# The last feed-forward's first four feature blocks: computed with tokens in rows from eight 512-column weight units, six of them converted before the sub-layer starts

## The chip, the cores and the metric

The kernel runs on one core of a Trainium2 chip. The metric is the device time of one execution in microseconds (us). The engines named below are TensorE (PE, with its weight loads PEld), VectorE (DVE), ScalarE (ACT), and SyncE (SP), which issues nearly all loads.

## The reference, cut to what matters

A trunk of two layers works on 256 latent tokens and 256 context tokens, 1024 features each, in fp32. Each layer is a half-step SwiGLU feed-forward, a block of parallel token mixers, and another half-step feed-forward:

```
def swiglu(x, w_gate, w_up, w_down):
    return (jax.nn.silu(x @ w_gate) * (x @ w_up)) @ w_down

def modulated_norm(x, mod, k, norm_g):
    return rms_norm(x, norm_g[2 * k]) * (1 + mod[:, :, 3 * k + 1]) + mod[:, :, 3 * k]

def gated_residual(x, y, mod, k, norm_g, weight):
    return x + weight * mod[:, :, 3 * k + 2] * rms_norm(y, norm_g[2 * k + 1])

def half_ffn(x, mod, k, norm_g, w):
    h = modulated_norm(x, mod, k, norm_g)
    return gated_residual(x, swiglu(h, *w), mod, k, norm_g, FFN_RESIDUAL)
```

The feed-forward has 2816 hidden features. Only the latent stream is returned, so the last mixer's second half and the last feed-forward run on the 256 latent tokens alone.

## The kernel before, in words

**Arithmetic.** Every fp32 operand of a large product is split into a high and a low part. ACT rounds it to the high part (line 162 for weights, 188 for activations), DVE subtracts that from the original (lines 163 and 189). `mm3` then makes three matmuls of each product, high by high, high by low and low by high (lines 193 to 195).

**Weights** come in units of 512 KB, [128 partitions, 1024 floats]. `run_tasks` walks a list of tasks, each with the units it needs. It loads up to three units ahead into four `raw` buffers (SP, line 152) and converts two ahead into five `hi` and five `lo` buffers. Larger activations live in 13 "slots" of 2064 floats per partition.

**Order.** Each engine takes its instructions in the order of its queue. That order is fixed when the program is built: a scheduler places instructions by the order in which they are written, and what stands under `urgent()` is put earlier, past other work that is ready. SP's loads are one such queue: a load that waits for its buffer holds up the loads behind it.

**The stretch of the change** is the end of the second layer's mixer and the start of the last feed-forward. The 256 tokens are two blocks of 128, tb0 and tb1.

- The mixer's merge makes u (`uhi`, `ulo`) from eight feature blocks. Then the residual X is loaded back from memory into a slot (`unspill`, line 883).
- `closing` makes the out-projection: tb0's first 512 columns (4 units, 24 matmuls of 512 columns), the second 512 columns of tb0 and then of tb1 (4 units held for both), and tb1's first 512 columns (4 units again). That is 96 matmuls.
- After each block's second half comes its chain: the square sums (ACT line 561), the product with the gate (DVE 563), 1/sqrt in small DVE steps (570, 210 to 219), the residual (DVE 574), the next norm's square sum (ACT 446), 1/sqrt again, and the normalised rows xn (DVE 451).
- `prenorm` turns xn to feature rows by 16 transposes on PE (line 468), four to a PSUM tile, each tile with two features of both blocks. It scales and shifts them 256 columns at a time (DVE 476, ACT 478) and splits them. With one stream `turn()`, which calls `prenorm`, stands behind tb1's chain, since each tile needs both blocks.
- The feed-forward then runs one weight unit per task: `gu(f, w)` holds 128 features of the gate (w = 0) or up (w = 1) weights as PE's stationary operand and streams the 256 tokens, 24 matmuls of 256 columns. silu is on ACT (603), the product on DVE (606). Eight such units make the first four of 22 feature blocks.

## Time and profile before

| what | value |
|---|---|
| median of three runs | 2246.11 us (2245.7 to 2246.91) |
| the profiled execution | 2245.83 us |
| its span in the trace | 2244.0 us |
| mean granted TensorE clock | 0.992 |
| PE busy | 97% of the span |
| DVE, ACT busy | 69%, 44% of the span |

The span is the part of the execution that the trace covers. [...] The "busy" shares are means over very different stages, so the stretch of the change has to be read by itself.

### The profile page before, as it was taken

To read this page: it belongs to the slowest core of one execution; us is meant where nothing else is said; L and a number is where in the kernel's file an instruction comes from. 1 tells how busy PE (TensorE), PEld (TensorE's weight loads), DVE (VectorE), ACT (ScalarE), POOL (GpSimd) and SP (SyncE) were. 2 spreads that over 40 slices of the span, in tenths; PEclk is the share of its full clock that TensorE was granted. 3 is DMA by queue.
4 is the path that set the end of the run, shared out by engine and by line. 5 is a ranking of instruction groups with operands and counts; after the bars stand their busy time and mean duration, and the time that the engine had idled before them with its cause. 6 is when DMAs were issued, how large, how long until landed. Compare 5 with 4: busy or idle time off the path is not lost.

```text
span 2244.0 us, 30646 instructions
## 1 busy us (share of the span) xinstructions
PE 2186.8 (97%) x11666; PEld 1833.2 (82%) x11666; DVE 1546.0 (69%) x2760; ACT 997.9 (44%) x1594; POOL 135.4 (6%) x100
## 2 busy tenths in 40 slices
PE   7999999999999999999999999999999999998998
PEld 4877777787888888888878788777778888997997
DVE  4987775778576775664444378878858887876556
ACT  3322223545577833542222253222236468855444
POOL 0000000013152000000000000000000152000000
PEclk9999999999999999999999999999999999998999
DMA  7765564321213334434434236555744214565664
GB/s 285 226 197 182 165 200 146 123 94 68 92 51 113 122 120 143 142 112 133 139 104 134 101 118 197 189 187 181 222 138 152 85 67 126 183 217 173 193 190 155
DMA packets 127555, 334.52 MB, mean 149 GB/s; under 512 B 12840, under 2 KB 26216, under 8 KB 126640
## 3 DMA queue, kind: packets, MB, share of 16 engines
q1 hardware_dynamic: 112240, 315.60, 43.4%
q10 hardware_dynamic: 15168, 16.97, 2.4%
q8 instruction: 91, 1.49, 0.3%
q14 instruction: 56, 0.46, 0.1%
HBM read 322.48 MB, written 10.04 MB: 148 GB/s over the span
## 4 chain that ended last, share of the span: by engine, by line
PE 89%; DVE 6%; ACT 2%; issue 1%; DMA 1%; ACTq 0%; DVEq 0%
PE ps L193 27%; PE ps L194 27%; PE ps L195 27%; PE ps L1259 1%; PE ps L1058 1%; PE ps L1228 1%; PE ps L366 1%; DVE lo L163 1%; PE ps L1073 1%; PE ps L468 1%; PE ps L1075 1%; PE ps L1016 1%; DVE sm L1020 1%; DMA slot<-in_w_ada_dram 1%; PE ps L1019 1%
## 5 line engine op out<-in xcount | busy, mean ns | idle before, releaser
L162 ACT ACTIVATE hi<-raw 128x1024 fp32r<-128x1024 f32 (+1 forms) x444 | 457.4, 1032 | 770.7 <-PE ps L194 255.9
L193 PE MATMUL ps<-slot,hi 128*128 128x512 f32 (+1 forms) x2232 | 778.4, 351 | 6.0 <-ACT slot L188 4.9
L194 PE MATMUL ps<-slot,hi 128*128 128x512 f32 (+1 forms) x2232 | 775.6, 348 | 0.7 <-DVE slot L189 0.5
L195 PE MATMUL ps<-slot,lo 128*128 128x512 f32 (+1 forms) x2232 | 773.6, 347 | 0.0
L163 DVE TENSOR_TENSOR lo<-raw,hi 128x1024 fp32r<-128x1024 f32 (+1 forms) x444 | 526.7, 1190 | 232.3 <-ACT hi L162 230.6
L193 PEld LDWEIGHTS ps<-slot,hi 128*128 128x128 f32 x2232 | 420.5, 189 | 75.9 <-ACT slot L188 6.2
L195 PEld LDWEIGHTS ps<-slot,lo 128*128 128x128 f32 x2232 | 421.5, 189 | 57.4
L194 PEld LDWEIGHTS ps<-slot,hi 128*128 128x128 f32 x2232 | 421.5, 189 | 56.3 <-DVE slot L189 2.0
L193 PE MATMUL ps<-hi,slot 128*128 128x512 f32 (+2 forms) x1048 | 400.3, 382 | 1.9 <-ACT slot L188 1.1
L195 PE MATMUL ps<-hi,slot 128*128 128x512 f32 (+2 forms) x1048 | 398.8, 381 | 0.0
L194 PE MATMUL ps<-lo,slot 128*128 128x512 f32 (+2 forms) x1048 | 398.8, 381 | 0.0
L358 DVE SCALAR_TENSOR_TENSOR t<-raw,sc,t 128x1024 f32<-128x1024 f32 x224 | 280.3, 1281 | 129.9 <-DMA raw<-in_w_ada_dram 129.7
L1046 POOL TENSOR_SCALAR t<-t,sm 128x512 f32<-128x512 f32 (+1 forms) x96 | 135.2, 1420 | 1748.1 <-DVE sm L1043 1693.2
L193 PEld LDWEIGHTS ps<-hi,slot 128*128 128x128 f32 x1048 | 197.1, 188 | 46.2 <-issue 6.6
L195 PEld LDWEIGHTS ps<-hi,slot 128*128 128x128 f32 x1048 | 196.7, 188 | 39.8
L194 PEld LDWEIGHTS ps<-lo,slot 128*128 128x128 f32 x1048 | 197.0, 188 | 38.9 <-issue 0.2
L188 ACT ACTIVATE slot<-t 128x512 fp32r<-128x512 f32 (+1 forms) x138 | 80.5, 594 | 172.3 <-DVE t L606 153.5
L606 DVE TENSOR_TENSOR t<-ps,t 128x512 f32<-128x512 f32 (+1 forms) x88 | 54.7, 622 | 86.5 <-PE ps L195 85.2
L189 DVE TENSOR_TENSOR slot<-t,slot 128x512 fp32r<-128x512 f32 (+1 forms) x138 | 87.6, 643 | 5.1 <-ACT slot L188 4.6
L1020 DVE TENSOR_REDUCE sm<-ps 128x1 f32<-128x512 f32 (+1 forms) x96 | 54.1, 593 | 29.6 <-PE ps L1019 29.0
L603 ACT ACTIVATE t<-ps 128x512 f32<-128x512 f32 (+1 forms) x88 | 46.4, 527 | 24.2 <-DVE t L426 16.5
L189 DVE TENSOR_TENSOR t<-ps,t 128x512 fp32r<-128x512 f32 x80 | 54.2, 684 | 1.9 <-ACT t L188 1.7
(195 smaller groups left out, 1667.7 us busy)
## 6 DMA issues: line engine op xcount, KB each, us to landing
raw<-in_w_gu_dram SPq DMA_DIRECT2D x176, 512.0 KB
raw<-in_w_ada_dram SPq DMA_DIRECT2D x128, 512.0 KB
raw<-in_w_down_dram SPq DMA_DIRECT2D x92, 512.0 KB
raw<-in_w_fm_dram SPq DMA_DIRECT2D x64, 512.0 KB
raw<-in_w_br_dram SPq DMA_DIRECT2D x24, 512.0 KB
raw<-in_w_out_dram SPq DMA_DIRECT2D x24, 512.0 KB
slot<-in_w_ada_dram SPq DMA_DIRECT2D x16, 512.0 KB
raw<-in_w_down_dram SPq DMA_DIRECT2D x20, 256.0 KB
```

Source lines behind the costliest of these rows:

```text
L162: self.nc.scalar.activation(out=hi, in_=raw, func=AF.Copy)
L163: self.nc.vector.tensor_tensor(out=lo, in0=raw, in1=hi.bitcast(F32), op=ALU.subtract)
L188: self.nc.scalar.activation(out=hi, in_=src, func=AF.Copy)
L189: self.nc.vector.tensor_tensor(out=lo, in0=src, in1=hi.bitcast(F32), op=ALU.subtract)
L193: mm(out, lh, rh, start=start, stop=False, **kw)
L194: mm(out, lh, rl, start=False, stop=False, **kw)
L195: mm(out, ll, rh, start=False, stop=stop, **kw)
L358: v.scalar_tensor_tensor(out=acc, in0=units[0], scalar=c, in1=acc, op0=ALU.mult, op1=ALU.add)
L603: nc.scalar.activation(out=hs["sg"][:, :W], in_=ps[:, :W], func=AF.Silu)
L606: nc.vector.tensor_tensor(out=hid[:, :W], in0=ps[:, :W], in1=hid[:, :W], op=ALU.mult)
L1020: v.tensor_reduce(out=mx[:, e:e + 1], in_=ps[:, :nkey], axis=AX.X, op=ALU.max)
L1046: nc.gpsimd.tensor_scalar(out=t[:, :nkey], in0=t[:, :nkey], scalar1=r[:, e:e + 1], scalar2=None, op0=ALU.mult)
```

## The change

- The feed-forward's first eight `gu` units are replaced by eight `gt` units from a new weight array, the first 512 gate and then up columns, in pieces of two 128-feature input blocks by 512 columns.
- `rows_first` takes the tokens of one block as stationary operand and streams the weights: 48 matmuls of 512 columns for tb0, then `pre(1)`, which is tb1's norm, then 48 for tb1. A block's product is [128 tokens, 512 features]. silu and the product act on it whole, four transposes turn it to feature rows, and it is split straight from PSUM.
- `prenorm_block` makes the norm of one token block: two PSUM tiles of four transposes each, each scaled in four pieces of 128 x 128 (two on DVE, two on ACT), then split. It is urgent. `turn()` is called ahead of the last two out-projection tasks of tb1.
- The first six `gt` units are loaded and converted ahead into slots, three among the last merge tasks and three among tb0's first out-projection tasks. The last two come through the ordinary `hi` and `lo` buffers.
- `pair` lays a high and a low part of 256-token width into one slot. u, the last feed-forward's input and its hidden features take half the slots, and the six units take the slots set free.

```
+    def pair(self, W):
+        if 8 * W > SLOT:
+            return self.slot([P, 4, W], F32R), self.slot([P, 4, W], F32R)
+        t = self.slot([P, 2, 4, W], F32R)
+        return t[:, 0], t[:, 1]
...
+    def prenorm_block(self, l, k, tb, st):
...
+        with self.urgent():
+            for c4 in range(2):
+                pt = self.psum()
+                h = self.t512()
+                for i in range(4):
+                    nc.tensor.transpose(pt[:, i * P:(i + 1) * P], xn[:, (4 * c4 + i) * P:(4 * c4 + i + 1) * P], self.ident)
+                for i in range(4):
+                    o, p = h[:, i * P:(i + 1) * P], pt[:, i * P:(i + 1) * P]
...
+                    if i % 2:
+                        nc.scalar.activation(out=o, in_=p, func=AF.Identity, scale=sc, bias=sh)
+                    else:
+                        nc.vector.tensor_scalar(out=o, in0=p, scalar1=sc, scalar2=sh, op0=ALU.mult, op1=ALU.add)
+                sl = slice(tb * P, (tb + 1) * P)
+                self.split(st["hi"][c4][:, :, sl], st["lo"][c4][:, :, sl], h.rearrange("p (c t) -> p c t", c=4))
...
-                if i == nu - TURN and tbs is gb and len(streams) > 1:
+                if i == nu - TURN and tbs is gb:
                     turn()
...
+            def rows_first(units, hs=hs):
+                units = list(rest) + list(units)
+                for tb in range(2):
+                    if tb:
+                        pre(tb)
+                    pss = [self.psum() for _ in range(2)]
+                    sl = slice(tb * P, (tb + 1) * P)
+                    for n, u in enumerate(units):
+                        w, g = divmod(n, 4)
+                        for x in range(2):
+                            kk = 2 * g + x
+                            self.mm3(pss[w], st["hi"][kk // 4][:, kk % 4, sl], st["lo"][kk // 4][:, kk % 4, sl],
+                                     u[0][:, x, :], u[1][:, x, :], kk == 0, kk == NK - 1)
...
+                    g = self.t512()
+                    nc.scalar.activation(out=g, in_=pss[0], func=AF.Silu)
+                    nc.vector.tensor_tensor(out=g, in0=pss[1], in1=g, op=ALU.mult)
+                    pt = self.psum()
+                    for f in range(4):
+                        nc.tensor.transpose(pt[:, f * P:(f + 1) * P], g[:, f * P:(f + 1) * P], self.ident)
+                    self.split(hs["hi"][0][:, :, sl], hs["lo"][0][:, :, sl], pt.rearrange("p (f t) -> p f t", f=4))
...
-        out += mrg[2]
+        early = [[t] for t in ahead]
+        out += weave(mrg[2], sum(early[:3], []))
...
+        end = self.closing(st, qs, False, keys, mm, done, turn)
+        return out + weave(end[:4], sum(early[3:], [])) + end[4:]
```

Where the order moves, first on SP around the load of X (`slot` from `spill`). Before, it stands behind the fourth out-projection unit:

```order
L152 DMA raw_17386<-in_w_fm_dram 128x1024
L152 DMA raw_17388<-in_w_out_dram 128x2x512
L152 DMA raw_17440<-in_w_out_dram 128x2x512
L152 DMA raw_17494<-in_w_out_dram 128x2x512
L152 DMA raw_17496<-in_w_out_dram 128x2x512
L883 DMA slot_17594<-spill_84 128x2048
L152 DMA raw_17546<-in_w_out_dram 128x2x512
```

After the change:

```order
L163 DMA raw_17492<-in_w_out_dram 128x2x512
L163 DMA raw_17501<-in_w_out_dram 128x2x512
L163 DMA raw_17503<-in_w_gt_dram 128x1024
L163 DMA raw_17553<-in_w_out_dram 128x2x512
L163 DMA raw_17603<-in_w_gt_dram 128x1024
L163 DMA raw_17612<-in_w_out_dram 128x2x512
L945 DMA slot_17607<-spill_84 128x2048
L163 DMA raw_17625<-in_w_gt_dram 128x1024
L163 DMA raw_17636<-in_w_out_dram 128x2x512
```

Three `gt` units now stand among the out-projection's loads, the last of them between X and the fifth out-projection unit. X's slot was fresh before. After the change it is one of those that held the mixer's normalised input, which PE reads until the last of the merge's gate products.

On DVE, at the out-projection of tb0, before (189 is the last split of u, 163 a unit's low part, 563 the two halves of tb0 multiplied with the gate):

```order
L189 TENSOR_TENSOR slot_17391<-slot_16182,slot_17390 128x256
L163 TENSOR_TENSOR lo_17651<-raw_17613,hi_17650 128x1024
L163 TENSOR_TENSOR lo_17655<-raw_17625,hi_17654 128x1024
L563 TENSOR_TENSOR slot_17648<-ps_17602,slot_17592 128x512
L163 TENSOR_TENSOR lo_17659<-raw_17637,hi_17658 128x1024
L563 TENSOR_TENSOR slot_17648<-ps_17674,slot_17592 128x512
```

And after (204, 178 and 599 are the same three lines):

```order
L204 TENSOR_TENSOR slot_17393<-slot_16182,slot_17393 128x256
L178 TENSOR_TENSOR slot_17650<-raw_17625,slot_17650 128x1024
L178 TENSOR_TENSOR lo_17656<-raw_17636,hi_17655 128x1024
L599 TENSOR_TENSOR slot_17670<-ps_17614,slot_17605 128x512
L178 TENSOR_TENSOR lo_17673<-raw_17642,hi_17672 128x1024
L178 TENSOR_TENSOR lo_17679<-raw_17653,hi_17678 128x1024
L178 TENSOR_TENSOR lo_17683<-raw_17659,hi_17682 128x1024
L178 TENSOR_TENSOR lo_17687<-raw_17676,hi_17686 128x1024
L599 TENSOR_TENSOR slot_17670<-ps_17702,slot_17605 128x512
```

Before, the seventh to ninth out-projection units (of twelve) are converted between the last split of u and the second 563. After, the sixth `gt` unit and the fifth to ninth out-projection units are. Between that second product and tb0's xn (451 before, 466 after) stand eight more conversions in both kernels.

On PE, between tb0's and tb1's matmuls, after the change (208 to 210 are the three matmuls of `mm3`, 701 turns tb0's hidden features, 512 turns tb1's norm):

```order
L208 MATMUL ps_17910<-hi_17891,slot_17815 128x512
L209 MATMUL ps_17910<-lo_17892,slot_17815 128x512
L210 MATMUL ps_17910<-hi_17891,slot_17815 128x512
L701 MATMUL ps_17964<-ident,t_3122_17961 128x128
L512 MATMUL ps_17971<-ident,t_3108_17889 128x128 x4
L512 MATMUL ps_17983<-ident,t_3108_17889 128x128 x4
L701 MATMUL ps_17964<-ident,t_3122_17961 128x128 x3
L208 MATMUL ps_17995<-slot_17271,slot_17814 128x512
```

Before, there is no such place: all transposes of the norm (468) stand ahead of the first feed-forward matmul, and 192 matmuls follow without one between. Now the first of the transposes of tb0's hidden features stands ahead of those of tb1's norm, and all twelve ahead of tb1's first matmul.

On DVE at the end of the new part, after the change (698 is the product of silu and up for tb1, 519 a scale step, 204 a split):

```order
L519 TENSOR_SCALAR t_3127_17984<-ps_17983,Amod_8896,modT_8895 128x128
L204 TENSOR_TENSOR slot_17814<-t_3125_17972,slot_17814 128x4x128
L204 TENSOR_TENSOR slot_17815<-t_3127_17984,slot_17815 128x4x128
L178 TENSOR_TENSOR lo_18089<-raw_17905,hi_18088 128x1024
L698 TENSOR_TENSOR t_3130_18045<-ps_17996,t_3130_18045 128x512
L178 TENSOR_TENSOR lo_18123<-raw_17907,hi_18122 128x1024
L204 TENSOR_TENSOR slot_17959<-ps_18048,slot_17959 128x4x128
```

The conversion of the second `gu` unit that follows (`lo_18089`) stands ahead of tb1's product. On PE, tb1's four transposes (701) stand behind that product and ahead of the next units' matmuls.

## Rows read from the trace of the kernel before

**Rows 1.** The page, busy time of each engine (share of the span).

```profile
PE 2186.8 (97%) x11666; PEld 1833.2 (82%) x11666; DVE 1546.0 (69%) x2760; ACT 997.9 (44%) x1594; POOL 135.4 (6%) x100
```

**Rows 2.** The page, the chain of work that ended last, by engine.

```profile
PE 89%; DVE 6%; ACT 2%; issue 1%; DMA 1%; ACTq 0%; DVEq 0%
```

**Rows 3.** Waits of PE from 1850 us: us in total, times, longest.

```profile
PE ps L468 <- DVE t L451: 11.2, 2, 6.3
```

**Rows 4.** PE's timeline: start, us, instructions, [idle before <- releaser].

```profile
2013.98 0.39 PE L193 MATMUL ps<-hi,slot 128*128 128x512 f32 x1
...
2035.97 0.39 PE L195 MATMUL ps<-hi,slot 128*128 128x512 f32 x1
2042.65 1.11 PE L468 MATMUL ps<-ident,t 128*128 128x128 f32 x4 [6.29 <-DVE t L451]
2048.63 2.82 PE L468 MATMUL ps<-ident,t 128*128 128x128 f32 x12 [4.87 <-DVE t L451]
2051.43 1.44 PE L193 MATMUL ps<-slot,hi 128*128 128x256 f32 x5
2052.66 0.37 PE L194 MATMUL ps<-slot,hi 128*128 128x256 f32 x1
```

**Rows 5.** DVE's timeline, the chains of tb0 and tb1.

```profile
2026.01 0.69 DVE L563 TENSOR_TENSOR slot<-ps,slot 128x512 f32<-128x512 f32 x1 [2.67 <-ACT t L561]
...
2037.41 0.68 DVE L563 TENSOR_TENSOR slot<-ps,slot 128x512 f32<-128x512 f32 x1
...
2041.84 0.75 DVE L451 TENSOR_SCALAR t<-slot,sm 128x1024 f32<-128x1024 f32 x1
...
2047.82 0.75 DVE L451 TENSOR_SCALAR t<-slot,sm 128x1024 f32<-128x1024 f32 x1
```

**Rows 6.** Instruction groups from 1900 to 2060: busy us, mean ns, idle before.

```profile
L163 DVE TENSOR_TENSOR lo<-raw,hi 128x1024 fp32r<-128x1024 f32 x48 | 58.3, 1222 | 12.8 <-ACT hi L162 12.6
L162 ACT ACTIVATE hi<-raw 128x1024 fp32r<-128x1024 f32 x48 | 50.7, 1058 | 27.9 <-PE ps L194 9.2 <-issue 5.7 <-DMA raw<-in_w_om_dram 2.7
...
L1241 ACT ACTIVATE t<-slot,ZN 128x128 f32<-128x128 f32 x38 | 13.0, 388 | 0.0
...
L189 DVE TENSOR_TENSOR slot<-t,slot 128x512 fp32r<-128x512 f32 x6 | 4.1, 689 | 0.7 <-ACT slot L188 0.6
...
L188 ACT ACTIVATE slot<-t 128x512 fp32r<-128x512 f32 x6 | 3.7, 629 | 2.3 <-DVE t L990 2.3
...
L1270 DVE TENSOR_SCALAR slot<-ps,sm 128x128 f32<-128x128 f32 x8 | 2.8, 344 | 0.0
```

**Rows 7.** SP's timeline: issues of X's load and of out-projection units.

```profile
2003.20 0.46 SPq L883 DMA_DIRECT2D slot<-spill  x1
2007.81 13.42 SPq L152 DMA_DIRECT2D raw<-in_w_out_dram  x8
```

**Rows 8.** Windows: us, busy us by engine, PEclk, DMA share, GB/s.

```profile
2003.00:2011.00 8.00, 8.00 (x70) 8.00 (x69) 5.86 (x10) 4.52 (x7) 0.00 (x0) 1.00 0.90 326
2011.00:2020.00 9.00, 9.00 (x54) 7.87 (x52) 7.04 (x11) 6.57 (x9) 0.00 (x0) 1.00 0.71 237
```

**Rows 9.** Windows with the granted clock (PEclk), the closing and an earlier stage.

```profile
2039.00:2040.00 1.00, 0.00 (x0) 0.00 (x0) 1.00 (x1) 0.87 (x1) 0.00 (x0) 0.60 0.77 274
2040.00:2052.00 12.00, 4.49 (x18) 3.71 (x19) 9.12 (x28) 3.15 (x7) 0.00 (x0) 0.50 0.36 122
2052.00:2053.00 1.00, 1.00 (x8) 1.00 (x7) 0.72 (x3) 1.00 (x3) 0.00 (x0) 0.57 0.00 0
...
528.00:530.00 2.00, 2.00 (x7) 1.55 (x7) 1.10 (x2) 1.11 (x2) 2.00 (x2) 0.50 0.80 287
...
1799.00:1801.00 2.00, 2.00 (x16) 1.78 (x15) 1.92 (x7) 1.17 (x4) 0.72 (x1) 1.00 0.00 0
```

**Rows 10.** PE's timeline, two gaps of nearly equal length.

```profile
526.49 0.39 PE L1073 MATMUL ps<-t,slot 128*128 128x256 f32 x1 [2.18 <-ACT t L1034]
...
1798.31 0.39 PE L1073 MATMUL ps<-t,slot 128*128 128x256 f32 x1 [2.19 <-DVE t L189]
```

More of the change, by code (lines that the diff above doesn't have):

```diff
@@ L46 @@
 N_HI = 5
+N_EARLY = 6
 LA_DMA = 3
@@ L159, in cvt_unit @@
         n = int(np.prod(shape))
-        hi = self.wp.tile([P, n], F32R, tag="hi", name=self.nm("hi"))
-        lo = self.wp.tile([P, n], F32R, tag="lo", name=self.nm("lo"))
+        if key[0] == "gt" and key[4]:
+            both = self.slot([P, 2, n], F32R)
+            hi, lo = both[:, 0, :], both[:, 1, :]
+        else:
+            hi = self.wp.tile([P, n], F32R, tag="hi", name=self.nm("hi"))
+            lo = self.wp.tile([P, n], F32R, tag="lo", name=self.nm("lo"))
         self.nc.scalar.activation(out=hi, in_=raw, func=AF.Copy)
@@ L177, in run_tasks @@
                     nd += 1
-                ready[ncv] = self.cvt_unit(raws.pop(ncv))
+                ready[ncv] = self.cvt_unit(raws.pop(ncv), keys[ncv])
                 ncv += 1
@@ L483, in prenorm @@
             self.split(dh, dl, hv)
+    def prenorm_block(self, l, k, tb, st):
+        nc = self.nc
+        M = self.L[l]
+        if "hi" not in st:
+            st["hi"], st["lo"] = zip(*[self.pair(2 * P) for _ in range(2)])
+        xn = st["xn"][tb]
+        with self.urgent():
[6 more added lines that the diff above has]
+                    o, p = h[:, i * P:(i + 1) * P], pt[:, i * P:(i + 1) * P]
+                    sc, sh = M["A"][:, k, 4 * c4 + i, 0:1], M["modT"][:, 6 * k + c4, i, 0:1]
+                    if i % 2:
+                        nc.scalar.activation(out=o, in_=p, func=AF.Identity, scale=sc, bias=sh)
+                    else:
+                        nc.vector.tensor_scalar(out=o, in0=p, scalar1=sc, scalar2=sh, op0=ALU.mult, op1=ALU.add)
+                sl = slice(tb * P, (tb + 1) * P)
+                self.split(st["hi"][c4][:, :, sl], st["lo"][c4][:, :, sl], h.rearrange("p (c t) -> p c t", c=4))
     def y_half(self, st, tb, n):
@@ L534, in fn @@
                     post(tbs, 0, tbs is gb)
-                    if tbs is gb and len(streams) == 1:
-                        turn()
             return ([keys[0][i]], fn)
@@ L591, in open_hidden @@
                 if "hi" not in hs:
-                    hs["hi"] = [self.slot([P, 4, W], F32R) for _ in range(2)]
-                    hs["lo"] = [self.slot([P, 4, W], F32R) for _ in range(2)]
+                    hs["hi"], hs["lo"] = zip(*[self.pair(W) for _ in range(2)])
             def mms(ps, u, a, b, kks=range(NK), start=True, **kw):
@@ L643, in early_half @@
                 return fn
+            def rows_first(units, hs=hs):
[11 more added lines that the diff above has]
+                                     u[0][:, x, :], u[1][:, x, :], kk == 0, kk == NK - 1)
+                    if not tb:
+                        open_hidden(hs)
+                    g = self.t512()
[5 more added lines that the diff above has]
+                    self.split(hs["hi"][0][:, :, sl], hs["lo"][0][:, :, sl], pt.rearrange("p (f t) -> p f t", f=4))
             first = 0
+            if part == 0 and len(streams) == 1:
+                first = 8
+                out.append(([("gt", l, n // 4, n % 4, False) for n in range(N_EARLY, 8)], rows_first))
             if part == 0 and len(streams) > 1:
@@ L828, in k_cols, with mixer_tasks @@
             R["K"].append(K)
-    def mixer_tasks(self, l, need_ctx, ms, pre, done, turn):
+    def mixer_tasks(self, l, need_ctx, ms, pre, done, turn, ahead):
         nc = self.nc
@@ L942, in mm @@
                 self.mm3(ps, lh, ll, u[0][:, x, :], u[1][:, x, :], k == 0, k == NK - 1)
-        return out + self.closing(st, qs, False, keys, mm, done, turn)
+        end = self.closing(st, qs, False, keys, mm, done, turn)
+        return out + weave(end[:4], sum(early[3:], [])) + end[4:]
     def conv_task(self, l, c, ms, R, need_ctx):
@@ L1342, in fn @@
                 if n == 2 and j % 4 == 0:
-                    R.setdefault("uhi", []).append(self.slot([P, 4, W], F32R))
-                    R.setdefault("ulo", []).append(self.slot([P, 4, W], F32R))
+                    for q, t in zip(("uhi", "ulo"), self.pair(W)):
+                        R.setdefault(q, []).append(t)
                 units = list(units)
@@ L1419, in turn @@
         return (lambda: pre(n + 1)(0)) if n < 5 else (lambda: None)
+    early_units = []
+    ahead = [([("gt", 1, n // 4, n % 4, True)], lambda units: early_units.extend(units)) for n in range(N_EARLY)]
     B.consts()
@@ L1432 @@
         if kind == "mix":
-            tasks += B.mixer_tasks(l, l == 0, states[n], pre(n), done(n), turn(n))
+            tasks += B.mixer_tasks(l, l == 0, states[n], pre(n), done(n), turn(n), [] if l == 0 else ahead)
             continue
-        sub = B.ffn_tasks(l, k // 2, k, streams(n), states[n], pre(n), done(n), turn(n), first[1] if n == 0 else None, rest)
+        sub = B.ffn_tasks(l, k // 2, k, streams(n), states[n], pre(n), done(n), turn(n), first[1] if n == 0 else None, rest if n == 0 else early_units)
         head = 4 if n else 4 + 1 + 3 * FIRST + len(first[1])
@@ L1466, in _layout @@
     a["w_gu"] = c(gu.reshape(2, 2, 2, NK, P, NF, P).transpose(0, 1, 5, 2, 4, 3, 6))
+    gt = np.stack([f["ffn_w_gate"][1, 1, :, :512], f["ffn_w_up"][1, 1, :, :512]])
+    a["w_gt"] = c(gt.reshape(2, NK, P, 512).transpose(0, 2, 1, 3))
     a["w_down"] = f["ffn_w_down"]
```

7 lines of the change are left out of this document (6 added, 1 removed).

## The prediction

> **What bounds the kernel now.** The engine shares come first: PE is busy 97% of the span [rows 1], and the chain that ended last runs 89% on PE [rows 2]. So time is gained only where PE waits, or where it does less work. PE's work doesn't shrink: before, the eight units are 192 matmuls of 256 columns, after, 96 of 512. What is left is PE's waiting, so the waits of PE are read next. In the last 394 us PE waits 11.2 us for xn, in two waits [rows 3]. The timeline places them: 6.29 us ahead of the first four transposes and 4.87 us ahead of the other twelve [rows 4].
>
> All times below are counted from T0 = 2013.98, the first out-projection matmul [rows 4]. The 96 matmuls of 512 columns start 0.2315 us apart ((2035.97 - 2013.98) / 95), and 256 columns take half of that, 0.1157. So before, the out-projection ends at T0+22.2, the first feed-forward matmul starts at T0+37.45 (2051.43), and the eight units end at 2052.66 + 187 x 0.1157 = 2074.3, T0+60.3. This last point is the same point in both programs, because the same `gu` units follow. I work out where it lands.
>
> Why PE waits is in DVE's timeline: tb0's second half is multiplied with its gate at 2026.01, and xn of tb0 is done at 2042.59 [rows 5]. Between stand eight conversions of 1.22 us each [rows 6], 9.8 of 16.6 us. The first wait is DVE's queue. The second is tb1's chain: 2037.41 to 2048.57, 11.2 us [rows 5].
>
> **Supply of the out-projection.** X's load was issued at 2003.20, T0-10.8 [rows 7]. Now its slot is free only after the last merge block's gate product has read it. That block is 24 gate matmuls and then 12 more of 256 columns, so the slot comes free between T0-2.8 and T0-1.4. SP's queue stands still until then, and behind X wait the sixth `gt` unit and the fifth out-projection unit. These 2.1 MB take 6.4 us at the 326 GB/s seen when X and units were loaded together [rows 8], and land at T0+3.6 to 5.0. Conversion adds 1.06 on ACT and 1.22 on DVE [rows 6]: T0+5.9 to 7.3. PE wants it at about T0+5.8 (after 24 matmuls). I take a stall of 0.85 us. The bounds are 0 and, at the 237 GB/s of the next window [rows 8] (8.9 us), 4.0.
>
> **tb0's chain.** In the built order five matmuls of tb1 stand among tb0's second half. It ends at T0+11.1+1.15+0.85 = T0+13.1, where it was T0+11.1. From there to xn it took 17.5 us, and I take 17.0, since the same eight conversions still stand between and DVE has less slack. So xn is ready at T0+30.1. The out-projection ends at T0+23.05. **PE's first wait isn't removed: 7.1 us for 6.3.** Packing and early units don't touch it, since the conversions that fill DVE here are those of later units.
>
> **tb0's norm.** The clock has fallen to 0.50 in the first wait before [rows 9], and does so again. Eight transposes at half clock take 1.9 (2.82 / 12 each [rows 4]). Then come the scale steps: two of 0.344 on DVE beside two of 0.388 on ACT per tile (nearest rows, 128 x 128 [rows 6]), which adds about 0.75 behind the last transpose. The split is 0.63 and 0.69 [rows 6]. In sum 3.95 us: matmuls run from T0+34.1. The bounds are 2.8 (what it took before from twelve transposes to the first matmul [rows 4]) and 5.0, since the out-projection's second product of tb1 (0.68 [rows 5]) and its square sum stand in between. Here is the gain: from xn to the first matmul was 8.85 us, with tb1's chain inside, and is 3.95, so **-4.9**.
>
> [...]
>
> **tb0's matmuls.** 48 x 0.2315 = 11.1. Before, PE ran steadily from 2048.63 and the clock was full at about 2052.66, 4.0 us later [rows 4, 9]. I take the same 4.0 us at half clock, which costs 2.0. So tb0 ends at T0+47.2. tb1's chain hides behind it: its gate product now stands behind three scale steps of tb0 (about T0+32.8), plus 11.2 is T0+44. The second wait is gone.
>
> **The gap to tb1.** PE's next instruction is the first transpose of tb0's hidden features. It needs the product of up with silu, a 128 x 512 step from PSUM (0.69 [rows 5]): PE is idle 0.75 us. Behind it in the queue stand tb1's eight norm transposes, though xn has been ready for 3 us, and three more: twelve, 1.35 us. Then PE waits for two scale steps and the split, 0.69 + 0.63 + 0.69, 2.05 us. So the new gap is 4.15 us, with 2.8 idle, and tb1 runs from T0+51.35 to T0+62.45. The bounds are 2.7 (the high part alone, scale steps hidden) and 5.5 (scale and split of both tiles one after the other).
>
> **The clock in that gap.** Two gaps of 2.18 and 2.19 us ended differently: behind one the clock was 0.50, behind the other 1.00 [rows 9, 10]. This gap is longer in sum but broken by transposes. If it drops, 4 us at half clock cost 2.1. I take the drop, because 2.8 of 4.15 us are idle. [...]
>
> **The tail.** Before, the next units' matmuls follow without a gap. Now tb1's four transposes stand ahead of them. They need the product (0.69), which on DVE stands behind a conversion whose `hi` buffer comes free only 6 matmuls (1.4 us) before tb1's end: 1.06 + 1.22 ends 0.9 after it. Then 0.69 and four transposes, 0.46: 2.05 us, so T0+64.5. Bounds 1.2 (no conversion) and 3.0.
>
> **The sum.** tb0's first matmul 3.35 earlier (T0+34.1 for 37.45), which is -4.9 and 1.55 of lateness. Then: more half clock (2.0, before about 0.6 in the matmuls) +1.4, the gap +4.1, the tail +2.05. That is T0+64.5 for 60.3, **+4.2**; with the clock's drop in the gap **+6.3**. Behind this point PE didn't wait before, and the units are the same. In the merge PE is saturated, and the three early conversions there fit beside it (ACT idle, DVE busy 5.86 of 8.0 us [rows 8]); without that cover each costs up to 1.22. The profiled execution took 2245.83 us, which makes 2252.1; the median shown lies 0.28 higher, so 2252.4.
>
> **The rivals.**
>
> - *A, the forecast*: the clock drops in the gap, 2252.4. Chance 0.40.
> - *B, no drop there*: 2250.3. For it, the 2.19 us gap without one. Chance 0.25.
> - *C, supply*: X's load (1 MB) and three `gt` units (1.5 MB) more in the closing slow all units. At 237 GB/s the fifth unit comes 2.5 us later, and with it tb0's whole chain: 2254 to 2257. For it, the DMA share was 0.90 when X was loaded [rows 8]; against, it was 0.71 in the next 9 us. Chance 0.12.
> - *D, the small losses stay near their lower bounds*: no stall (-0.85), first matmul after 2.8 (-1.15), gap 2.7 (-1.4), tail 1.2 (-0.8), no drop: 2246.1 to 2247, no change. Each has a row for it, but all have to hold. Chance 0.13.
> - *E, the other side*: the eight conversions no longer hold up tb0's xn. Without them the chain is 17.5 - 9.8 = 7.7 us, xn is ready at T0+20.8, before the out-projection ends, so the first wait goes, and the clock stays full: PE starts tb0 at T0+26 (-8.1, and -2.0 of half clock). That gives 2240 to 2242. It decides at T0+23: xn ready before or after. For it, DVE waited 12.8 us for high parts in this part of the trace [rows 6], so conversions could run earlier, where it idles; against, the eight conversions still stand ahead of xn in DVE's queue. Chance 0.10.
>
> **How the numbers follow.** A tells slower from no change at 0.2% (4.5 us, what a measurement of this kernel can tell) in most of its spread (0.35 of 0.40), B in a little under half (0.11 of 0.25), C always. D is mostly no change. Slower 0.58, same 0.31, faster 0.11. The range runs from D's lower end to C's, 2245.3 to 2256.5; E and C's far end are left out.
>
> **What would show it.** PE's wait for xn of tb0 stays near 7 us (E: gone), and the second wait of 4.87 is missing. Between tb0's and tb1's products stand about 4 us with twelve transposes, and behind tb1 a wait of 1.6 us for the product. The clock is 0.50 for some 4 us behind tb0's start, and again behind the gap (A) or not (B). A wait of PE for a low part near T0+6 shows the stall. The prediction is wrong if xn of tb0 comes before T0+26, or if a wait outside this stretch changes by over 2 us.

## The result, and the profile after

| kernel | median us | runs | profiled span us |
|---|---|---|---|
| before | 2246.51 (2245.7 to 2248.2) | 4 | 2244.0 |
| after | 2262.55 (2260.84 to 2264.49) | 4 | 2259.1 |

The change makes the kernel slower: ratio 1.0064, interval 1.0052 to 1.0077, which is 11.7 to 17.3 us; the two medians of the table lie 16.0 apart. The forecast was slower by 6, so the sign was right and the size was not.

The page of the kernel after has nearly the same shares as [rows 1, 2]: busy time of each engine, then the chain that ended last.

```profile
PE 2194.8 (97%) x11578; PEld 1834.7 (81%) x11578; DVE 1546.8 (68%) x2760; ACT 997.3 (44%) x1594; POOL 134.8 (6%) x100
PE 87%; DVE 6%; ACT 2%; DMA 2%; issue 2%; ACTq 0%; POOL 0%; DVEq 0%; POOLq 0%
```

PE is still the bound, and DMA has come up to 2% of the chain. The waits of PE from 1850 us show where (total, times, longest); they answer to [rows 3]:

```profile
PE ps L512 <- DVE t L466: 7.2, 1, 7.2
PE ps L208 <- ACT slot L203: 4.2, 2, 2.1
PE ps L701 <- DVE t L698: 2.5, 2, 1.6
PE ps L208 <- ACT hi L177: 1.4, 1, 1.4
PE ps L209 <- DVE lo L178: 0.5, 1, 0.5
...
```

The second wait for xn is gone, as it was meant to be. In its place stand two waits for the split norm (L203), two for the hidden product (L698) and two for a converted weight unit (L177, L178). PE's timeline, which answers to [rows 4], places them:

```profile
2016.41 0.39 PE L208 MATMUL ps<-hi,slot 128*128 128x512 f32 x1
...
2021.76 0.39 PE L210 MATMUL ps<-hi,slot 128*128 128x512 f32 x1
2023.58 0.73 PE L208 MATMUL ps<-hi,slot 128*128 128x512 f32 x2 [1.43 <-ACT hi L177]
2024.84 0.55 PE L209 MATMUL ps<-lo,slot 128*128 128x512 f32 x1 [0.53 <-DVE lo L178]
2025.20 0.63 PE L210 MATMUL ps<-hi,slot 128*128 128x512 f32 x1
...
2042.53 0.39 PE L210 MATMUL ps<-hi,slot 128*128 128x512 f32 x1
2050.15 1.97 PE L512 MATMUL ps<-ident,t 128*128 128x128 f32 x8 [7.23 <-DVE t L466]
2054.20 0.80 PE L208 MATMUL ps<-slot,slot 128*128 128x512 f32 x1 [2.08 <-ACT slot L203]
...
2067.53 0.40 PE L210 MATMUL ps<-hi,slot 128*128 128x512 f32 x1
2068.78 0.33 PE L701 MATMUL ps<-ident,t 128*128 128x128 f32 x1 [0.85 <-DVE t L698]
2068.95 1.04 PE L512 MATMUL ps<-ident,t 128*128 128x128 f32 x8
2069.82 0.49 PE L701 MATMUL ps<-ident,t 128*128 128x128 f32 x3
2072.39 0.50 PE L208 MATMUL ps<-slot,slot 128*128 128x512 f32 x1 [2.08 <-ACT slot L203]
...
2084.92 0.40 PE L210 MATMUL ps<-hi,slot 128*128 128x512 f32 x1
2086.93 0.66 PE L701 MATMUL ps<-ident,t 128*128 128x128 f32 x4 [1.62 <-DVE t L698]
2087.34 0.36 PE L208 MATMUL ps<-slot,hi 128*128 128x256 f32 x1
```

T0 is 2016.41 here. The clock, by windows of the same trace (us, busy us by engine, PEclk, DMA share, GB/s), as [rows 9]:

```profile
2016.00:2025.00 9.00, 7.04 (x32) 5.11 (x32) 7.77 (x11) 6.24 (x10) 0.00 (x0) 1.00 0.91 328
2026.00:2028.00 2.00, 2.00 (x6) 1.57 (x5) 1.89 (x2) 1.09 (x2) 0.00 (x0) 0.50 0.76 261
2029.00:2045.00 16.00, 13.92 (x60) 10.91 (x59) 12.59 (x20) 9.33 (x11) 0.00 (x0) 1.00 0.79 279
2046.00:2059.00 13.00, 6.77 (x19) 5.37 (x20) 9.83 (x28) 5.41 (x12) 0.00 (x0) 0.50 0.35 115
2073.00:2076.00 3.00, 3.00 (x9) 2.35 (x8) 0.75 (x2) 0.35 (x1) 0.00 (x0) 0.50 0.01 3
```

The clock is at its lower level (0.50, with matmuls of 512 columns 0.43 us apart instead of 0.23) three times: behind the waits at T0+7, behind the long wait for xn, and behind the gap to tb1. Put side by side, all from each program's own T0 (the forecast is its case A):

| point | before | forecast | after | after less forecast |
|---|---|---|---|---|
| out-projection ends | 22.2 | 23.05 | 26.35 | +3.3 |
| first norm transposes | 28.67 | 30.1 | 33.74 | +3.6 |
| first feed-forward matmul | 37.45 | 34.1 | 37.79 | +3.7 |
| tb0's matmuls end | | 47.2 | 51.35 | +4.15 |
| tb1's first matmul | | 51.35 | 55.98 | +4.6 |
| the eight units are done | 60.3 | 66.6 | 70.9 | +4.3 |
| end of the span | 230.0 | 236.3 | 242.7 | +6.4 |

So from T0 the kernel after is 12.7 us longer: 10.6 in the stretch and 2.1 in what follows it. The two spans differ by 15.1, because T0 itself is 2.4 later (2016.41 for 2013.98). At least 2.0 of these aren't the change's. The last 1000 matmuls ahead of T0, in whose time the three early units of the merge are loaded and converted, take 131.8 us in both kernels, so these units cost nothing there, as forecast. The 2.0 arise further back, at the gap of 2.19 us near 1798 us that [rows 10] show: behind it the clock stayed at 1.00 in the profiled execution of before and fell to 0.50 in that of after. The same gap ends both ways without any change to it. The program of `e9_rows_close` (below) is that of before up to the last feed-forward's input, and in its execution the clock fell (PE's timeline and a window):

```profile
1800.33 0.39 PE L1074 MATMUL ps<-t,slot 128*128 128x256 f32 x1 [2.18 <-DVE t L189]
1801.00:1804.00 3.00, 3.00 (x12) 2.52 (x12) 1.75 (x6) 1.19 (x4) 1.71 (x2) 0.50 0.00 0
```

All 17 profiles of this case have this gap; the clock fell behind it in 10 and not in 7. So times are compared from T0, and the time from T0 to the end of the span is given for each experiment.

### The profile page after: what moved, and what is told of

The parts are those of the page before. It is cut to its first block, busy times and chain, and to the rows that moved or that the text cites. A ratio compares the mean times of both kernels' runs of the same rounds, so it can differ in the third digit from the quotient of the medians.

```text
span 2259.1 us, 30459 instructions
## 1 busy us (share of the span) xinstructions
PE 2194.8 (97%) x11578; PEld 1834.7 (81%) x11578; DVE 1546.8 (68%) x2760; ACT 997.3 (44%) x1594; POOL 134.8 (6%) x100
## 4 chain that ended last, share of the span: by engine, by line
PE 87%; DVE 6%; ACT 2%; DMA 2%; issue 2%; ACTq 0%; POOL 0%; DVEq 0%; POOLq 0%
PE ps L208 27%; PE ps L209 27%; PE ps L210 26%; PE ps L1323 1%; PE ps L1122 1%; PE ps L1292 1%; DVE lo L178 1%; PE ps L381 1%; DMA raw<-in_w_out_dram 1%; PE ps L1137 1%; ACT hi L177 1%; PE ps L1139 1%; DVE sm L1084 1%; PE ps L1080 1%; PE ps L1083 1%
## 5 line engine op out<-in xcount | busy, mean ns | idle before, releaser
L177 ACT ACTIVATE hi<-raw 128x1024 fp32r<-128x1024 f32 (+1 forms) x438 | 450.8, 1031 | 763.0 <-PE ps L209 253.3
L208 PE MATMUL ps<-slot,hi 128*128 128x512 f32 (+1 forms) x2168 | 760.8, 352 | 6.0 <-ACT slot L203 4.9
L209 PE MATMUL ps<-slot,hi 128*128 128x512 f32 (+1 forms) x2168 | 758.8, 350 | 1.1 <-DVE slot L204 0.9
L210 PE MATMUL ps<-slot,lo 128*128 128x512 f32 (+1 forms) x2168 | 756.3, 349 | 0.0
L178 DVE TENSOR_TENSOR lo<-raw,hi 128x1024 fp32r<-128x1024 f32 (+1 forms) x438 | 519.4, 1189 | 235.9 <-ACT hi L177 234.1
L208 PEld LDWEIGHTS ps<-slot,hi 128*128 128x128 f32 x2168 | 407.8, 189 | 75.5 <-issue 6.7
L210 PEld LDWEIGHTS ps<-slot,lo 128*128 128x128 f32 x2168 | 409.2, 189 | 57.4
L209 PEld LDWEIGHTS ps<-slot,hi 128*128 128x128 f32 x2168 | 409.2, 189 | 56.6 <-DVE slot L204 2.3
L203 ACT ACTIVATE slot<-t 128x512 fp32r<-128x512 f32 (+1 forms) x134 | 79.0, 600 | 181.4 <-DVE t L641 161.5
```

Source lines behind the costliest of these rows:

```text
L177: self.nc.scalar.activation(out=hi, in_=raw, func=AF.Copy)
L178: self.nc.vector.tensor_tensor(out=lo, in0=raw, in1=hi.bitcast(F32), op=ALU.subtract)
L203: self.nc.scalar.activation(out=hi, in_=src, func=AF.Copy)
L208: mm(out, lh, rh, start=start, stop=False, **kw)
L209: mm(out, lh, rl, start=False, stop=False, **kw)
L210: mm(out, ll, rh, start=False, stop=stop, **kw)
```

## The experiments

Before's median beside the runs of this section is 2248.1 to 2248.4 us; ratios are to it. Diffs are to the kernel after unless they say "to before". The experiments ran on four chips, each beside before; where the kernel after was measured, before took 2246.51.

**Three early units instead of six** (`e6_early3`) asks whether the stall is a matter of how much is loaded.

```
-N_EARLY = 6
+N_EARLY = 3
```

> The changed kernel with only three units converted ahead, those among the merge; the other five go through the ordinary five hi and lo buffers, so no extra unit passes the four raw buffers during the out-projection. X's load stays late. Theory after the second run (the three extra units of the closing and their turn through four raw buffers starve the out-projection): PE's waits near T0+6 fall to under 0.5 us, the clock stays 1.00 there and the time falls by 3 to 4 us, to about 2259. Rival (X's late load alone holds SP's queue): the waits stay at 1.5 to 2 us and the time within 1 us of 2262.5.

Measured: 2254.22 us, ratio 1.003 (1.0021 to 1.0039), 234.2 from T0. PE's waits in the stretch:

```profile
PE ps L512 <- DVE t L466: 6.6, 1, 6.6
PE ps L208 <- ACT slot L203: 4.2, 2, 2.1
PE ps L701 <- DVE t L698: 2.5, 2, 1.6
```

No wait for a converted unit is left, and the out-projection ends at T0+22.31, 4.0 earlier than after, with X's load still late (issued at T0-2.4). From T0 this kernel is 8.5 shorter than after, the largest single piece; 1.2 of that lies behind the stretch (see the distance of matmuls below). It took with it a part that I hadn't expected. The gap to tb1 has the same two waits in both kernels, but here the clock stays full behind it. From tb1's first matmul to its hidden transposes are 13.0 us here and 14.5 after. PE's timeline:

```profile
2062.80 0.33 PE L701 MATMUL ps<-ident,t 128*128 128x128 f32 x1 [0.85 <-DVE t L698]
...
2066.40 0.50 PE L208 MATMUL ps<-slot,slot 128*128 128x512 f32 x1 [2.08 <-ACT slot L203]
...
2079.43 0.66 PE L701 MATMUL ps<-ident,t 128*128 128x128 f32 x4 [1.61 <-DVE t L698]
```

Its window behind the gap, with the clock as the third number from the end:

```profile
2068.00:2070.00 2.00, 2.00 (x11) 1.61 (x10) 0.09 (x1) 0.00 (x0) 0.00 (x0) 1.00 0.00 0
```

**X's load earlier, with six units** (`e2_x_early`) and **with three** (`e7_early3_x`). The first moves X five tasks forward, and with it one early unit from the merge into the closing:

```
-        out += weave(mrg[2], sum(early[:3], []))
-        out += self.gate_task(l, 1, qs) + [([], unspill)]
+        tail = weave(mrg[2], sum(early[:2], []))
+        if ahead:
+            tail[-5:-5] = self.gate_task(l, 1, qs) + [([], unspill)]
+            out += tail
...
-        return out + weave(end[:4], sum(early[3:], [])) + end[4:]
+        return out + weave(end[:4], sum(early[2:], [])) + end[4:]
```

The second has `N_EARLY = 3` and all three units in the merge.

> The changed kernel with X's load put five tasks earlier, so that X has the fresh slot and the third early unit (now in the closing) takes a slot of the mixer's input instead; SP's queue no longer stands still. Theory (X's late load starves the out-projection's fifth unit, and the short wait drops TensorE's clock): PE's waits of 1.43 and 0.53 us near T0+6 go, the clock stays 1.00 there, the out-projection ends at T0+22.5 instead of T0+26.5, and the time falls by about 4 us to 2258.5. Rival (the loads are limited by the rate of the DMA engines or by raw buffers, not by SP's wait): the wait stays at 1 to 2 us and the time within 1 us of the changed kernel.

> As the run before with three early units, and X's load five tasks earlier as well. If either cause alone (extra units, or X) makes the waits near T0+6, they are gone here, the out-projection takes 22.2 to 22.5 us instead of 26.5, and the time is about 4 us under the changed kernel, 2258.5. If only this run loses the waits and the one before doesn't, both have to go together.

Measured: 2261.98 us, ratio 1.0058 (1.0044 to 1.0072), 246.2 from T0; and 2254.95 us, 1.0031 (1.002 to 1.0042), 234.1 from T0. With six units the waits for converted weights grew, 3.6 us for high parts and 0.8 for a low part, and the out-projection ended at T0+29.61. With three units nothing changed against `e6_early3`. An early X doesn't remove the stall. That it would do nothing by itself isn't shown, since one unit moved with it in the first.

**tb1's norm inside tb0's matmuls** (`e3_pre_mid`):

```
-                    if tb:
-                        pre(tb)
...
+                        if tb == 0 and n == 6:
+                            pre(1)
```

> The changed kernel with tb1's norm called after six of tb0's eight units instead of after all eight. Theory (the gap is only PE's order: xn of tb1 is ready 6 us before tb0 ends): the gap of 4.9 us between tb0's and tb1's matmuls shrinks to 1 us of transposes within them, the clock doesn't drop behind it (1.9 us), and the time falls by 5 to 6 us to about 2257. Rival (the gap is tb0's product and tb1's scale and split, which then only wait elsewhere): a wait of 2 us or more shows up ahead of tb1's first matmul or of tb0's transposes, and the time falls by less than 3.

Measured: 2257.07 us, ratio 1.0034 (1.0022 to 1.0046), 8.8 over its before where after was 16.0 over, 238.9 from T0 (3.8 less than after). PE's timeline:

```profile
2064.73 1.04 PE L512 MATMUL ps<-ident,t 128*128 128x128 f32 x8
2070.28 0.66 PE L701 MATMUL ps<-ident,t 128*128 128x128 f32 x4 [0.78 <-DVE t L698]
```

And its window behind that:

```profile
2072.00:2076.00 4.00, 4.00 (x19) 3.26 (x18) 0.30 (x1) 0.00 (x0) 0.00 (x0) 1.00 0.00 0
```

The norm's transposes now run between tb0's matmuls, and its scale steps and split behind them. Of the gap only the 0.78 us for the product and four transposes are left, and the clock stays full. So the gap came from where the norm was written.

**Low parts of the last four units left out** (`e10_no_low`). Their low part is the high part again, so a part of the products is missing.

```
...
+        if key in [("gt", 1, 1, 2, False), ("gt", 1, 1, 3, False), ("gu", 1, 1, 4, 0), ("gu", 1, 1, 4, 1)]:
+            return v(hi), v(hi)
         self.nc.vector.tensor_tensor(out=lo, in0=raw, in1=hi.bitcast(F32), op=ALU.subtract)
```

> The changed kernel without the low part of the last four units that are converted ahead during the out-projection (their high part is used in its place, so part of the product is left out); PE's and ACT's work is the same and four conversions of 1.2 us are gone from DVE's queue ahead of tb0's xn. Theory (the first wait is DVE's queue): xn of tb0 is ready 4 to 5 us sooner after the out-projection's end, the wait falls from 7.2 to 2 to 3 us, the clock may stay full behind it, and the time falls by 4 to 7 us, to 2256 to 2258. Rival (the chain's own steps set it): the wait stays over 5.5 us and the time within 2 us.

Measured: 2257.84 us, ratio 1.0044 (1.003 to 1.0058), 238.3 from T0, 4.4 less than after. PE's timeline:

```profile
2043.23 1.09 PE L514 MATMUL ps<-ident,t 128*128 128x128 f32 x8 [2.63 <-DVE t L468]
```

Four steps of 1.22 us less on DVE, 4.9, and the wait for xn falls by 4.6 (7.23 to 2.63), though the out-projection ends where it did (T0+26.45). That wait is DVE's queue of conversions.

**These low parts on GpSimd** (`e8_pool`), meant to free DVE without leaving work out:

```
+        late = [("gt", 1, 1, 2, False), ("gt", 1, 1, 3, False), ("gu", 1, 1, 4, 0), ("gu", 1, 1, 4, 1)]
+        eng = self.nc.gpsimd if key in late else self.nc.vector
+        eng.tensor_tensor(out=lo, in0=raw, in1=hi.bitcast(F32), op=ALU.subtract)
```

> The changed kernel with the low parts of the last four units that are converted ahead during the out-projection made on GpSimd instead of DVE, so that three instead of eight conversions stand ahead of tb0's xn in DVE's queue. Theory (the first wait is DVE's queue of conversions): tb0's xn is ready 4 to 5 us sooner, the first wait falls from 7.2 to about 2.5 us and the clock may stay full; the time falls by 4 to 7 us, to about 2257. Rival (the chain's own steps and ACT's square sum set it): the wait stays over 5.5 us and the time within 2 us.

Measured: 2265.51 us, ratio 1.0078 (1.0064 to 1.0091), 246.6 from T0. The wait for xn grew to 10.3. GpSimd's and DVE's timelines:

```profile
2039.45 4.79 POOL L180 TENSOR_TENSOR lo<-raw,hi 128x1024 fp32r<-128x1024 f32 x2 [153.08 <-ACT hi L177]
2039.38 0.22 DVE L232 SCALAR_TENSOR_TENSOR sm<-sm,sm 128x1 f32<-128x1 f32 x1
2039.64 2.27 DVE L236 SCALAR_TENSOR_TENSOR sm<-sm,sm 128x1 f32<-128x1 f32 x1
2041.94 2.31 DVE L232 SCALAR_TENSOR_TENSOR sm<-sm,sm 128x1 f32<-128x1 f32 x1
2044.29 0.16 DVE L236 SCALAR_TENSOR_TENSOR sm<-sm,sm 128x1 f32<-128x1 f32 x1
```

A DVE step on one element per partition took 0.16 to 0.22 us, and 2.2 to 2.3 beside a GpSimd step. So DVE wasn't freed, and this run doesn't test the wait; `e10_no_low` does. The slow steps name two inputs (`sm<-sm,sm`). No step with one input stood beside a GpSimd step here, so what such a step would take isn't shown.

**The tail, tb1's hidden product behind the next unit** (`e5_tail`): silu, product and transposes of tb1 are written behind the first `gu` unit.

```
...
+                if q == first == 8:
+                    out.append(([], lambda _, hs=hs, fin=turn_hidden: fin(*hs.pop("held"), hs)))
```

> The changed kernel with tb1's silu, product, transposes and split written behind the first gate unit that follows, so that 24 matmuls cover them. Theory: the wait of 1.62 us for the product goes and the time falls by about 2 us to 2260.5. Rival (DVE's queue decides, and the transposes wait behind that unit as well): PE waits as long one unit later, and the time stays within 0.7.

Measured: 2262.99 us, ratio 1.0062 (1.0048 to 1.0076), 244.1 from T0 (1.4 more than after), no gain. The wait moved and grew, by PE's waits:

```profile
PE ps L707 <- DVE t L704: 3.7, 2, 2.9
```

silu now stood behind the `gu` unit's own silu on ACT, so its product came still later.

**Packing alone** (`e1_pack_only`, to before: only `pair` for u, the feed-forward's input and its hidden features) and **its row distance alone** (`e9_rows_close`, to before: the input in rows of 256 floats, in slots of its own).

```
-            st["hi"] = [self.slot([P, 4, T], F32R) for _ in range(2)]
-            st["lo"] = [self.slot([P, 4, T], F32R) for _ in range(2)]
+            st["hi"], st["lo"] = zip(*[self.pair(256 if (l, k) == (1, 2) else T) for _ in range(2)])
...
```

> The kernel before with nothing but the packing of high and low parts into one slot (u, the last feed-forward's input and hidden features). In the traces the 256-column matmuls behind the eight units start 0.117 us apart after the change and 0.115 before, which makes 1.8 us up to the end. If packing causes that, this kernel is 1.8 to 2.4 us slower than before, and its 256-column matmuls of the last feed-forward start 0.117 us apart. If it doesn't (rival: the difference is one of chips or runs), it is within 1 us of before and the distance is as in the kernel before on the same chip.

> The kernel before with the last feed-forward's input in four slots as before, but its four feature rows of 256 tokens close together (1 KB apart) instead of 2 KB apart; nothing is packed. Packing alone cost 3 us. If the distance of the rows causes it, this kernel is as slow as the packed one, 3 us over before, with 256-column matmuls 0.118 us apart. If sharing a slot by high and low part causes it, this kernel is as before, 0.115 us apart.

Measured: 2252.0 us, ratio 1.0014 (1.0004 to 1.0023), 233.9 from T0; and 2247.79 us, 0.9998 (0.999 to 1.0007), 230.2 from T0. Packing alone costs 3.9 from T0 without a new wait. What changed is the distance from one matmul of 256 columns to the next in the last feed-forward, worked out below from the starts of consecutive ones. The row distance isn't the reason.

**Other places for the same data** (`x1_slots64_w64`, `x2_slots64_w0`, `x3_slots0_w0`, to before): the slots lie 64 bytes further apart, and slots or weight buffers begin at other places in a partition. The room comes from fewer of the small buffers.

```
+        self.pad = self.wp.tile([P, 16], F32, tag="pad", name="pad", bufs=1)
...
-        return self.tp.tile([P, n], F32, tag="small", name=self.nm("sm"), bufs=16)
+        return self.tp.tile([P, n], F32, tag="small", name=self.nm("sm"), bufs=8)
...
-            R["RK"] = self.slot([P, SLOT])
+            R["RK"] = self.slot([P, SLOT + 16])[:, 0:SLOT]
```

This is the second. The first has no pad and `bufs=10`, and the third takes the pad from the slots' pool.

> The kernel before with the same instructions in the same order on every engine; only the slots' pitch is 8320 instead of 8256 bytes, so that every slot, and every raw, hi and lo buffer behind them, begins 64 bytes past a multiple of 128 (before, slots alternate between 0 and 64 and the buffers begin at 0). In the traces so far the 256-column matmuls of the last feed-forward start 115.3 ns apart where their streamed operand lies in slots at 64 (before, three early units), 118 to 119 where it lies at 0 or mixed (packed alone, the changed kernel). Theory A (the place of the streamed operand alone matters, packing doesn't): all such matmuls come at 115 ns and the kernel is 10 to 30 us faster than before. Theory B (what matters is that streamed operand and weights differ modulo 128): all come at 118 to 119 ns and it is 4 us or more slower. Rival (sharing a slot by high and low part is what costs, places don't): no change.

> As the run before, with the raw, hi and lo buffers at multiples of 128 again and all slots at 64. Theory A and theory B both say: all 256-column matmuls at 115 ns, 10 to 30 us faster than before. Rival (sharing a slot): no change.

> As the run before, with all slots and all raw, hi and lo buffers at multiples of 128. Theories A and B: 118 to 119 ns everywhere, 4 to 20 us slower than before. Rival (sharing a slot): no change.

Measured: 2250.87 us, ratio 1.0012 (1.0003 to 1.0021); 2245.76, 0.9992 (0.9983 to 1.0001); 2251.89, 1.0017 (1.0008 to 1.0026). Means over the starts from 2110 to 2230 us, where a gap counts if it has 105 to 130 ns:

| kernel | gaps | mean ns | from T0 us |
|---|---|---|---|
| before | 672 | 115.3 | 230.0 |
| e9_rows_close | 672 | 115.3 | 230.2 |
| e6_early3 | 672 | 115.9 | 234.2 |
| after | 664 | 117.8 | 242.7 |
| x2_slots64_w0 | 672 | 117.8 | 232.6 |
| e1_pack_only | 672 | 118.9 | 233.9 |
| x1_slots64_w64 | 672 | 120.0 | 234.7 |
| x3_slots0_w0 | 672 | 120.0 | 234.5 |

Before's last feed-forward has 1056 such matmuls (44 `gu` units of 24). At the mean's difference to 115.3 they make 2.6, 3.8, 5.0 and 5.0 us for the last four kernels, and from T0 those took 2.6, 3.9, 4.7 and 4.5 more than before. So the place of the data sets the price; the instructions and their order are the same in `x1`, `x2`, `x3` and before. `x2_slots64_w0` isn't slower by its median all the same: its T0 came at 2010.67, 3.3 earlier. Whether the new places gained that in earlier stages wasn't tried. Theories A and B both failed on `x2_slots64_w0` (115 expected, 117.8 measured), and the rival on all three. No rule of the addresses that I tried gives all the means. By the addresses of the built program, a streamed operand in the slot at byte 96320 of a partition gave 113.6 ns in before, unpacked, and 114.0 in `e6_early3`, packed; in the slot at 46784 it gave 117.2 and 117.8. So packing isn't what counts, but the rule of the places stays open.

**Three early units, the norm inside tb0, the product urgent and its transposes behind the first `gu` unit** (`b1`), then **the out-projection's first four units held for both blocks** (`b2`), and that **with six early units** (`b3`).

```
-N_EARLY = 6
+N_EARLY = 3
...
+                        if tb == 0 and n == 6:
+                            pre(1)
...
+                    with self.urgent():
+                        g = self.t512()
...
+                if q == first == 8:
+                    out.append(([], lambda _, hs=hs, fin=turned: fin(hs)))
```

These are `b1`'s; `b2` adds the lines below, and `b3` is `b2` with `N_EARLY = 6`.

```
+        joint = len(streams) == 1 and not add
...
+        if joint:
+            return [first(i) for i in range(nu)] + [(keys[1], both)]
```

> The changed kernel with three repairs: three early units instead of six, tb1's norm called after six of tb0's eight units, and tb1's hidden features turned behind the first gate unit that follows, with silu and product still at once. By the runs so far the first two are worth 8 and 6 us, the third 2 us if the product is no longer late: 2246 to 2248 on a chip where the kernel before takes 2248, no change against before. If the two gains are one and the same clock drop, 2250 to 2252.

> The three repairs of b1, and the out-projection's first four units used for both token blocks at once, so that four units fewer are loaded and converted. tb0's second half then ends 5.6 us later, but only four conversions stand behind it ahead of xn instead of eight. Theory (DVE's queue): the chain is 12.6 instead of 17 us, xn of tb0 comes at the same T0+29 and the time stays within 1 us of b1 (2249, the kernel before 2248). Rival (loads and their round trip set the chain): xn comes 2 us or more earlier and the time falls under 2246.

> As b2 but with six early units, as in the changed kernel: three extra units in the closing, four fewer out-projection units. Theory (the stall at T0+6 comes from the number of units that must pass the four raw buffers): the out-projection's units are needed half as fast, no wait of PE within it, and since only two gt units are left behind tb0's second half, the time is at or under b2. Rival (X's late slot alone stalls): PE waits 1 us or more within the out-projection, and the time is 2 to 4 us over b2.

| kernel | median us | ratio (interval) | from T0 us | out-projection ends | first transposes |
|---|---|---|---|---|---|
| b1 | 2249.01 | 1.0002 (0.9993 to 1.0011) | 230.7 | 22.31 | 29.18 |
| b2 | 2247.99 | 1.0002 (0.9993 to 1.0011) | 229.3 | 22.26 | 28.23 |
| b3 | 2250.17 | 1.0007 (0.9998 to 1.0016) | 231.5 | 22.25 | 28.18 |

`b3` has six early units and X as late as the kernel after, but four loads less, and its out-projection has no wait. So the stall comes with the number of units that must come through in time for the matmuls, not with X's late slot alone. `b3` is 2.2 slower than `b2` from T0, though it was expected at or under `b2`: its matmuls stand 117.8 apart for 115.9, and 864 of them make 1.6. None of the three beats the kernel before. But the loss of the stretch is gone: the first `gu` matmul behind the eight units starts at T0+60.3 in `b1`, for 60.4 before and 70.9 after, so the three repairs take away all of it. PE's waits of `b2` show what bounds this form:

```profile
PE ps L512 <- DVE t L466: 5.8, 1, 5.8
PE ps L208 <- ACT slot L203: 2.1, 1, 2.1
```

## Why the prediction was wrong in size

**Supply: the step that failed.** "I take a stall of 0.85 us" stood against 4.1: the out-projection took 26.35 for 22.2. By the starts of its matmuls 2.4 of that are the two waits (1.43 and 0.53 by the profile) with PE's start behind each. The other 1.7 are eight matmuls 0.427 apart instead of 0.2315, because the clock fell behind these waits (0.50 from 2026 to 2028 us). The loss doesn't hang on that drop. In `e5_tail`, whose instructions up to here are those of the kernel after, the clock stayed full, and waits alone took 3.85 by the starts, nearly as much: its out-projection ended at T0+26.06. Its waits, and its window behind them:

```profile
PE ps L209 <- DVE lo L178: 1.4, 2, 0.7
PE ps L208 <- ACT hi L177: 0.9, 1, 0.9
2025.00:2031.00 6.00, 5.91 (x24) 4.55 (x25) 4.58 (x5) 3.28 (x4) 0.00 (x0) 1.00 0.89 283
```

The bound for the wait alone, 4.0, would have held in both. What was wrong is the start of the 6.4 us. X's load was issued at T0-2.8 as worked out, but I let the two loads behind it start with it. The kernel after, by its timelines of SP, DVE (low parts) and ACT:

```profile
2013.65 0.34 SPq L945 DMA_DIRECT2D slot<-spill  x1
2015.91 0.34 SPq L163 DMA_DIRECT2D raw<-in_w_gt_dram  x1
2017.38 12.91 SPq L163 DMA_DIRECT2D raw<-in_w_out_dram  x8
2014.66 1.23 DVE L178 TENSOR_TENSOR lo<-raw,hi 128x1024 fp32r<-128x1024 f32 x1 [1.80 <-ACT hi L177]
2016.13 1.22 DVE L178 TENSOR_TENSOR slot<-raw,slot 128x1024 fp32r<-128x1024 f32 x1
2022.47 1.06 ACT L177 ACTIVATE hi<-raw 128x1024 fp32r<-128x1024 f32 x1 [0.39 <-DMA raw<-in_w_out_dram]
```

There are four `raw` buffers, and a buffer is free for the next load when DVE has made the low part of the unit in it. By the built program, the two low parts shown here set free the buffers of the sixth `gt` unit and of the fifth out-projection unit. They ended at 2015.89 and 2017.35, and SP issued the loads at 2015.91 and 2017.38, the second 3.7 us behind X. The fifth unit's high part, which waited for its load, began 5.1 us later, at T0+6.06. So 2.1 MB took 8.8 us. That is the time that 237 GB/s would have given, my slower rate, but that is luck: all loads together ran at 328. I blamed X's slot. `e2_x_early` and `e7_early3_x` say that an early X doesn't help, `e6_early3` and `b3` that fewer units through the raw buffers do. Fewer units are also fewer bytes, and no run has more raw buffers with the same loads, so how much is the buffers' part and how much the loads' isn't separated.

**A and C added up.** The clock fell in the gap to tb1 (A), and the supply was late by 3.3 beyond my sum (C). I had priced them as alternatives. Their sum, forecast 6.3 and 3.3 more, is 9.6 of the 10.6 measured in the stretch. The 3.3 passed on whole: tb0's first transposes were 3.6 late.

**The first wait.** Predicted 7.1, measured 7.23, for the reason given, though both its ends came over 3 us later than forecast: `e10_no_low` took away 4.9 us of conversions, and 4.6 of the wait went. Rival E was wrong, and D too: no loss but the one at tb1 came out below what I took.

**tb0's norm and matmuls.** From the first transpose to the first matmul 4.05 us (3.95); the matmuls 13.6 (13.1), the first of them at half clock as said (0.50 from 2046 to 2059 us). A scale step took 0.406 on DVE, for the 0.344 of the nearest row. DVE's group of them in the kernel after, with busy us, mean ns and idle before:

```profile
L519 DVE TENSOR_SCALAR t<-ps,Amod,modT 128x128 f32<-128x128 f32 x8 | 3.2, 406 | 2.6 <-PE ps L512 2.5
```

**The gap and the tail.** 4.6 us for 4.15, in the order foreseen, with twelve transposes; 2.2 for 2.05. `e3_pre_mid` shows the gap's cause. The tail's was read from the queue: DVE's product at 2086.19 stands behind the conversion at 2085.05. `e5_tail` only moved it.

**The clock in the gap.** It fell, as A says (0.50 from 2073 to 2076 us), and tb1 took 12.8 us (13.2). But `e6_early3` has the same gap with the clock full (1.00 from 2068 to 2070 us). Of the seven profiles with this gap the clock fell in the five with six early units (after, `e2_x_early`, `e5_tail`, `e8_pool`, `e10_no_low`; matmuls came to 0.43 us apart) and not in the two with three (`e6_early3`, `e7_early3_x`; 0.23); what decides it isn't shown. The two gaps of [rows 10], by which the prediction chose, couldn't tell: the one near 1798 us ends both ways in single executions of the same instructions. That A's drop came was partly luck, and a chance near one half was all that the rows gave. That the 2.8 us of idle time would bring it was my assumption, and isn't shown.

**Behind the stretch.** "PE didn't wait before, and the units are the same" was true, and 2.1 us were lost there. This is the second step that failed: the sum put that part at nothing. The 864 matmuls left are 117.8 apart for 115.3: 864 x 2.5 ns = 2.1. The new slot layout moved the streamed operand, and the sum had no term for it.

## What to carry to other kernels

Price the cases of a forecast as terms that can add up: a late supply and a clock drop came together here, and waits of 2.4 us on PE cost another 1.7 at half clock. When units are converted ahead, count every load that passes through the same raw buffers before the unit that PE needs next, and let each start when its buffer comes free, not with the load ahead of it. Two gaps in one profile don't show when the clock falls, since one and the same gap ended both ways in different executions. And a change of buffers is not free by itself: compare the distance between like matmuls before and after in a stage whose instructions didn't change.

## What the runs showed of the hardware

- Matmuls of 256 fp32 columns were 115.3 to 120.0 ns apart, by the place of the data in the partition, with the same instructions in the same order (`x1_slots64_w64`, `x3_slots0_w0`), which made up to 5 us in this feed-forward.
- A VectorE step of 128x1 with two inputs took 2.2 to 2.3 us instead of 0.16 to 0.22 beside a GpSimd step of 128x1024, which itself took 2.3 to 2.4 (`e8_pool`).
- Behind two waits of 1.43 and 0.53 us the clock was 0.50 for 3.4 us (the kernel after); behind three of 0.73, 0.92 and 0.72 us at the same place it stayed 1.00 (`e5_tail`). Behind a gap of 4.6 us with twelve transposes in it the clock was 0.50 in the kernel after and 1.00 in `e6_early3`.
- Behind one gap of 2.2 us, the same in all 17 programs, the clock fell to 0.50 in 10 profiled executions and stayed at 1.00 in 7.
